# A hybrid decoder layer: convolution taps, rotary adds, state arithmetic and roots of the mixing phase on other engines

## The chip, the cores and the metric

The kernel runs on one core of one Trainium2 chip. A core has TensorE (PE in the profile, with its weight loads as PEld), VectorE (DVE), ScalarE (ACT), GpSimd (POOL) and SyncE (SP); in this kernel nearly all transfers are issued from SP's queue. The metric is device time of one execution in microseconds: the median of several runs.

## The reference

One layer of a decoder with two kinds of heads side by side, on 2048 tokens of width 1024, in fp32. Cut to what matters here:

```
mod = silu(c) @ w_ada + b_ada                     # six rows of 1024: shift, scale, gate, twice
h = modulate(rmsnorm(x, norm1_w), shift1, scale1)
q, k, v, z, xbc, dt_raw = split(h @ w_in)         # one projection, cut into column groups
q, k = rope(q), rope(k)                           # t1*cos - t2*sin, t2*cos + t1*sin
attn = sliding_window_attention(q, k, v, sinks)   # window 128
xbc = silu(causal_depthwise_conv(xbc))            # four taps along the tokens, plus a bias
dt = softplus(dt_raw + dt_bias); a = dt * A
# the state recurrence (SSD), by chunks of 128 tokens:
xdt = xs * dt
y = (C.B * decay) @ xdt + C @ state * exp(a_cs)   # within the chunk, and from the state before
state = state * exp(a_total) + B @ (xdt * exp(a_cs_end - a_cs))
y = (y + xs * d_skip) * silu(z)
y = y * rsqrt(mean(y*y over groups of 256) + eps) * ssm_norm_w
x = x + gate1 * (concat(attn, y) @ w_out)
x = x + gate2 * swiglu(modulate(rmsnorm(x, norm2_w), shift2, scale2))
out = rmsnorm(x, final_norm_w)
```

## The kernel before

**Tiles and precision.** The tokens are worked in four blocks of 512 (b = 0 to 3), each of four tiles of 128 (token 0 to token 3 of a block, below, are such tiles). Every fp32 product is made of three fp32r products (`mm3`, L270 to L272: high by high, high by low, low by high), so each operand is split in two. A weight comes raw from DRAM through SP, ACT rounds it to its high half (L262), GpSimd or VectorE subtracts (L263), and the split pair is stored for the later blocks (L266) which load it whole (L258). A normalized token operand is made by L319 (VectorE), L321 (ACT) and L322 (VectorE) into tiles named `hl`.

**Stages.** After an opening come, block by block, the projections: queries (rotary embedding, L372 to L375), keys and values, convolution (L474 to L485) and gate (L491, L492), each written out to DRAM. Beside the projections of block b+1 run the mixing generators of block b: `attentions` (per tile: transposes, scores, softmax, values) and `ssds` (per tile: the state recurrence). A function `tick` takes 1.1 steps of these side generators per step of the main ones. So block 0 is mixed while block 1 is projected, and block 1 while block 2 is. The output projection and the feed-forward layer (L951 to L953, L1090) follow.

**A convolution chunk** (8 per block, 128 channels by 512 tokens) takes its product from a bank `d` of PSUM. GpSimd copies the three columns of the halo in and out (L474, L476), ACT copies the product (L475) and makes two taps into two tiles `s` (L478 with the bias, L479), VectorE adds a tap to each (L480 from PSUM, L481 from SBUF), GpSimd adds the two (L482), ACT takes tanh (L483), VectorE makes the product (L484).

**A tile of the state recurrence.** `factors` makes the decay's two operands of 128x512 from a triangle and the steps, the high one on VectorE (L690), the low one on GpSimd (L692). The four token transposes land in PSUM bank `st`; VectorE reads it twice (L724 with the step, L725 with the skip weight); GpSimd makes the decayed tokens from the first of these (L726). L755 (VectorE) scales the old state's output, L756 (GpSimd) adds the skip; L766 (GpSimd) decays the state, L767 (VectorE) adds to it. L776 and L777 finish the tile, L781 (ACT) sums squares, and the root over groups of 256 is taken by `rsqrt` (tile `rs`, scratch `rss`): L237 and L238 on VectorE make a first guess by integer arithmetic, and three Newton rounds, with L240 to L245, follow on GpSimd in thirteen operations (on VectorE the same function takes nine, L248 to L250). L788 (ACT) scales the tile, and four PE transposes (L709) turn it. Bank `st` is one buffer, and PE's next use of it is L736.

**The adaLN rows.** Of the 48 columns of `mod`, 32 are made while the blocks run: a column is two halves of 256 KB, each loaded by L189 into one of two buffers `aw` and reduced by one VectorE operation (L195, with a small read of its accumulator).

**What sets the order.** PE's order is the order of the program (a manual schedule). The order of VectorE, ACT, GpSimd and SP is set by a scheduler that simulates the program with its own durations when the kernel is built; so a change of one operation's engine can move others in these queues. Each engine runs its queue in order, and a queue's head that waits holds what is behind it, on SP the loads too.

Of the kernel before, what the change touches and what calls it, by code (L numbers as in the profile page):

```python
# [11 lines left out]
F32 = mybir.dt.float32  # L12
# [5 lines left out]
P = 128  # L18
# [3 lines left out]
T = 512  # L22
# [21 lines left out]
def hymba_layer(ctx, tc, xT, crow, pos, wada, wadk, vecs, rows, wq, wkv, wz, wx, wo, wgu, wd, outT):  # L44
# [318 lines left out]

    def rope(dst, src, heads, gt, eng=nc.gpsimd):
        s4 = src.rearrange("p (h two j) -> p h two j", two=2, j=HALF)
        d4 = dst.rearrange("p (h two j) -> p h two j", two=2, j=HALF)
        tm = big("s", 3, pool=fw)[:, :heads * 64]
        t4 = tm.rearrange("p (h two j) -> p h two j", two=2, j=HALF)
        c = cos[:, gt, :].unsqueeze(1).broadcast_to([P, heads, HALF])
        s = sin[:, gt, :].unsqueeze(1).broadcast_to([P, heads, HALF])  # L370
        for i in range(2):
            nc.vector.tensor_tensor(d4[:, :, i, :], s4[:, :, i, :], c, ALU.mult)  # L372
            nc.vector.tensor_tensor(t4[:, :, i, :], s4[:, :, 1 - i, :], s, ALU.mult)
        for i, op in ((0, ALU.subtract), (1, ALU.add)):
            eng.tensor_tensor(d4[:, :, i, :], d4[:, :, i, :], t4[:, :, i, :], op)  # L375

# [47 lines left out]
    def first_columns(h):  # L424
# [15 lines left out]
        for t, ps in enumerate(kb):  # L440
            key_value(0, t, ps, nc.vector)
        for t, ps in enumerate(qb):
            q = extra.m2()
            rope(q, ps, 8, t, nc.vector)
            nc.sync.dma_start(q_d[t], q)

    def key_value(b, t, ps, eng=nc.gpsimd):
        kv = staged()
        rope(kv[:, 0:P], ps[:, 0:P], 2, b * NT + t, eng)
        nc.scalar.copy(kv[:, P:2 * P], ps[:, P:2 * P])  # L450
        nc.vector.tensor_tensor(dt_of[b][:, t, :], ps[:, 2 * P:2 * P + 8], dt_bias, ALU.add)
        nc.sync.dma_start(kv_d[b * NT + t], kv)
# [9 lines left out]
    def convolved(b, h):  # L462
        for c in range(8):
# [9 lines left out]
            cin = small([P, T + 3], "cin", 2, pool=ip)  # L473
            nc.gpsimd.tensor_copy(cin[:, 0:3], halo[:, c, :])  # L474
            nc.scalar.copy(cin[:, 3:T + 3], ps)  # L475
            nc.gpsimd.tensor_copy(halo[:, c, :], cin[:, T:T + 3])  # L476
            cv, th, o = big("s", 3, pool=fw), big("s", 3, pool=fw), big("sx", 2, pool=ip)
            nc.scalar.activation(cv, cin[:, 0:T], AF.Identity, scale=conv_w[:, c, 0:1], bias=conv_b[:, c:c + 1])  # L478
            nc.scalar.activation(th, cin[:, 1:1 + T], AF.Copy, scale=conv_w[:, c, 1:2])  # L479
            nc.vector.scalar_tensor_tensor(cv, ps, conv_w[:, c, 3:4], cv, ALU.mult, ALU.add)  # L480
            nc.vector.scalar_tensor_tensor(th, cin[:, 2:2 + T], conv_w[:, c, 2:3], th, ALU.mult, ALU.add)  # L481
            nc.gpsimd.tensor_tensor(cv, cv, th, ALU.add)  # L482
            nc.scalar.activation(th, cv, AF.Tanh)  # L483
# [21 lines left out]
    def steps(b):  # L505
# [27 lines left out]
        ex = small([P, 3, NT, 8], "ex", 1)  # L533
        nc.scalar.activation(ex.rearrange("p k t h -> p (k t h)"), ps[:, 0:96], AF.Exp)
        return dt, ahi, alo, ex

# [68 lines left out]
    def load_values(kv, slot):  # L605
        v = kv[:, P:2 * P].rearrange("p (r d) -> p r d", d=64)
        vhi, vlo = (v_ring[:, at:at + 256].rearrange("p (r d) -> p r d", d=P)[:, :, 0:64]
                    for at in (slot * 192, (2 + slot) * 192))
        nc.scalar.copy(vhi, v)
        nc.gpsimd.tensor_tensor(vlo, v, vhi.bitcast(F32), ALU.subtract)  # L610

# [61 lines left out]
    def ssds(b, stepping, m):  # L673
# [10 lines left out]
        ub = upper.unsqueeze(1).broadcast_to([P, 4, P])  # L684
        dst, out = spill[b], None

        def factors(t, g):
            hs, u = slice(4 * g, 4 * g + 4), m.m4()
            uhi, ulo = u[:, 0, :], u[:, 1, :]
            nc.vector.tensor_tensor(uhi.rearrange("p (h l) -> p h l", h=4), ub,  # L690
                                    ahi[:, t, hs].bitcast(F32).unsqueeze(2).broadcast_to([P, 4, P]), ALU.mult)
            nc.gpsimd.tensor_tensor(ulo.rearrange("p (h l) -> p h l", h=4), ub,  # L692
                                    alo[:, t, hs].unsqueeze(2).broadcast_to([P, 4, P]), ALU.mult)
            return uhi, ulo
# [20 lines left out]
        for t in range(NT):  # L715
# [9 lines left out]
            nc.vector.tensor_tensor(by_head(xsd), by_head(ps), bc64(d_skip), ALU.mult)  # L725
            nc.gpsimd.tensor_tensor(by_head(xdte), by_head(xdt), bc64(edte), ALU.mult)  # L726
            ps = bank("sm", 1)
# [21 lines left out]
            if old is not None:  # L749
# [5 lines left out]
                nc.vector.tensor_tensor(by_head(y), by_head(yo), bc64(ecs), ALU.mult)  # L755
                nc.gpsimd.tensor_tensor(y, y, xsd, ALU.add)  # L756
            else:
# [7 lines left out]
            if old is not None:  # L765
                nc.gpsimd.tensor_tensor(by_head(new), by_head(old), bc64(etot), ALU.mult)  # L766
                nc.vector.tensor_tensor(new, new, st, ALU.add)  # L767
# [16 lines left out]
            rs = small([P, 2], "rs", 2)  # L784
            rsqrt(rs, ss, 2, nc.gpsimd, "rss", sb)
            for g in range(2):
# [878 lines left out]
```

## Time and profile before

| | |
|---|---|
| median of 3 runs | 2269.98 us (2266.66 to 2273.71) |
| the profiled execution | 2267.25 us, span 2265.4 us |
| mean granted clock of TensorE | 0.986 |
| moved by DMA | 470.45 MB, 208 GB/s over the span |

In the profile's groups stand a line of the program, the engine, the operation, output<-input and shapes, the count, then busy us and mean ns of one, then the idle time of the engine just ahead of these instructions and what ended it. In the list of waits the columns are the waiting engine and line, the engine and line waited for, us in total, number of waits and the longest. In the timeline they are start, duration, engine and line, with the idle time before in brackets. Of the page, the engines' busy share in 40 slices of 56.6 us, in tenths, and the granted clock, show that the whole first third is uneven:

```profile
PE   6888988999999999999999999998999999999998
DVE  8987976774549887788787768987777775776565
POOL 2655533545123311144342222222333331110021
PEclk9988999999999999999999999999999999999998
```

The slices 2 to 13, from about 57 to 740 us, are the blocks' projections with the mixing beside them; what follows is the feed-forward layer.

### The profile page before, as it was taken

The numbers are of one execution on the slowest core, as the hardware profiler recorded it, in microseconds if no ns is written. First come the engines' busy times: TensorE is split into PE (matmuls) and PEld (weight loads), VectorE is DVE, ScalarE is ACT, GpSimd is POOL, SyncE is SP. The second block draws the span as 40 slices with busy tenths as digits, with TensorE's granted clock in tenths as the row PEclk, the third lists the DMA queues.
The fourth block names the chain that finished last, engine by engine and source line by source line (L and its number), as shares of the span: only waits on it lengthen the run. The fifth ranks groups of instructions, "written<-read, shape, count | busy, mean of one in ns | idle before, by whom it ended". The sixth has DMA issues, their size and how long they took to land. (4 is left out here: it accounts for less than half of the span.)

```text
span 2265.4 us, 33515 instructions
## 1 busy us (share of the span) xinstructions
PE 2166.4 (96%) x11072; PEld 1801.9 (80%) x11072; DVE 1681.7 (74%) x3147; ACT 1008.4 (45%) x2113; POOL 700.2 (31%) x806
## 2 busy tenths in 40 slices
PE   6888988999999999999999999998999999999998
PEld 5778788888978888888888877777888888788887
DVE  8987976774549887788787768987777775776565
ACT  4564543665345655433344444532333333554342
POOL 2655533545123311144342222222333331110021
PEclk9988999999999999999999999999999999999998
DMA  8898988788879523234335579977333335777553
GB/s 296 293 318 298 319 259 258 252 265 271 291 244 339 198 91 110 94 117 126 94 103 182 190 259 310 328 225 227 125 98 105 98 91 197 270 261 268 171 168 100
DMA packets 289325, 470.45 MB, mean 208 GB/s; under 512 B 27392, under 2 KB 97024, under 8 KB 289152
## 3 DMA queue, kind: packets, MB, share of 16 engines
q1 hardware_dynamic: 288576, 467.80, 62.4%
q8 instruction: 87, 1.43, 0.3%
q14 instruction: 86, 0.70, 0.1%
q10 hardware_dynamic: 576, 0.52, 0.1%
HBM read 335.50 MB, written 132.71 MB: 207 GB/s over the span
## 5 line engine op out<-in xcount | busy, mean ns | idle before, releaser
L1090 PE MATMUL d<-a,w 128*128 128x512 f32 x1716 | 405.6, 396 | 7.0 <-DVE a L1062 3.9
L1090 PEld LDWEIGHTS d<-a,w 128*128 128x128 f32 x1716 | 321.6, 188 | 87.8 <-DVE a L1062 5.7
L951 PE MATMUL d<-b,w 128*128 128x512 f32 x924 | 366.0, 400 | 4.4 <-ACT t L975 4.4
L953 PE MATMUL d<-b,w 128*128 128x512 f32 x924 | 366.8, 398 | 1.9 <-DVE w L843 1.9
L952 PE MATMUL d<-b,w 128*128 128x512 f32 x924 | 367.5, 398 | 0.0
L280 POOL TENSOR_TENSOR acc<-acc,t 128x512 f32<-128x512 f32 x70 | 106.2, 1518 | 404.4 <-ACT t L279 389.8
L951 PEld LDWEIGHTS d<-b,w 128*128 128x128 f32 x924 | 174.5, 189 | 44.6 <-ACT t L975 5.5
L842 ACT ACTIVATE w<-s 128x512 fp32r<-128x512 f32 x176 | 110.8, 632 | 221.5 <-PE d L953 174.3
L953 PEld LDWEIGHTS d<-b,w 128*128 128x128 f32 x924 | 174.5, 189 | 42.5 <-DVE w L843 2.6
L952 PEld LDWEIGHTS d<-b,w 128*128 128x128 f32 x924 | 174.9, 189 | 38.6
L270 PE MATMUL d<-w,hl 128*128 128x256 f32 (+1 forms) x592 | 175.8, 297 | 6.9 <-ACT hl L321 4.5
L272 PE MATMUL d<-w,hl 128*128 128x256 f32 (+1 forms) x592 | 171.4, 289 | 1.8 <-DVE hl L322 1.8
L271 PE MATMUL d<-w,hl 128*128 128x256 f32 (+1 forms) x592 | 171.1, 289 | 0.0
L270 PE MATMUL d<-hl,w 128*128 128x512 f32 x352 | 146.3, 416 | 4.3 <-ACT w L262 2.2
L843 DVE TENSOR_TENSOR w<-s,w 128x512 fp32r<-128x512 f32 x176 | 143.2, 815 | 8.6 <-ACT w L842 7.3
L1086 DVE TENSOR_TENSOR w<-raw,w 128x512 fp32r<-128x512 f32 x156 | 107.2, 696 | 53.6 <-ACT w L1085 53.4
L272 PE MATMUL d<-hl,w 128*128 128x512 f32 x352 | 140.5, 399 | 1.4 <-DVE w L263 0.7
L842 ACT ACTIVATE w<-raw 128x512 fp32r<-128x512 f32 x132 | 82.9, 630 | 130.4 <-PE d L953 59.1
L271 PE MATMUL d<-hl,w 128*128 128x512 f32 x352 | 139.6, 397 | 0.0
L1085 ACT ACTIVATE w<-raw 128x512 fp32r<-128x512 f32 x156 | 90.7, 588 | 102.7 <-PE d L1090 67.5
L1062 DVE TENSOR_TENSOR a<-a 128x512 fp32r<-128x512 f32 x154 | 107.5, 720 | 37.3 <-ACT a L1061 37.0
L1005 POOL TENSOR_TENSOR t<-t 128x512 f32<-128x512 f32 x44 | 75.3, 1712 | 180.5 <-DVE t L1004 124.1
(414 smaller groups left out, 5017.7 us busy)
## 6 DMA issues: line engine op xcount, KB each, us to landing
raw<-in_wgu_dram SPq DMA_DIRECT2D x176, 256.0 KB, 2.9
w<-w_x SPq DMA_DIRECT2D x48, 512.0 KB, 5.1
act_t<-t SPq DMA_DIRECT2D x88, 256.0 KB, 3.3
a<-act_t SPq DMA_DIRECT2D x88, 256.0 KB, 4.8
t<-in_xT_dram SPq DMA_DIRECT2D x80, 256.0 KB, 4.2
act_b<-t SPq DMA_DIRECT2D x66, 256.0 KB, 2.2
a<-act_b SPq DMA_DIRECT2D x66, 256.0 KB, 5.0
aw<-in_wada_dram SPq DMA_DIRECT2D x64, 256.0 KB, 4.5
```

The costliest lines, as they stand in the source:

```text
L270: nc.tensor.matmul(out, ahi, bhi, start=first, stop=False)
L271: nc.tensor.matmul(out, ahi, blo, start=False, stop=False)
L272: mm3.last = nc.tensor.matmul(out, alo, bhi, start=False, stop=last)
L280: eng.tensor_tensor(acc, acc, sq, ALU.add)
L842: nc.scalar.activation(hi, x, AF.Copy)
L843: eng.tensor_tensor(lo, x, hi.bitcast(F32), ALU.subtract)
L951: nc.tensor.matmul(out, ahi, bhi, start=first and k == 0, stop=False, skip_group_check=True)
L952: nc.tensor.matmul(out, ahi, blo, start=False, stop=False, skip_group_check=True)
L953: mm3.last = nc.tensor.matmul(out, alo, bhi, start=False, stop=k == 3, skip_group_check=True)
L1062: nc.vector.tensor_tensor(lo, raw, hi.bitcast(F32), ALU.subtract)
L1086: nc.vector.tensor_tensor(w[1], raw, w[0].bitcast(F32), ALU.subtract)
L1090: mm3.last = nc.tensor.matmul(ps, w[x][:, ws], act[k][y][:, ts], start=new and k == 0 and x + y == 0, stop=k == KP - 1 and x == 1, skip_gr ...
```

## The change

Work of the mixing phase moves from GpSimd to VectorE or ACT.

- Rotary adds (L375): all on VectorE; before, those of block 0's first columns only.
- Convolution: the halo copies move to ACT. ACT's second tap and GpSimd's add go; VectorE adds the two middle taps one after the other to the tile that holds the first and last. Only one `s` tile takes sums now, the other holds tanh.
- The value's low half (L610): VectorE.
- Decayed tokens: VectorE makes them from the transposes in PSUM instead of GpSimd from `xdt`; the decay factor is multiplied by the step beforehand, once per block (one small VectorE product).
- For blocks 0 and 1 only: the low factor is four ACT activations of 128x128 instead of a GpSimd product of 128x512; the skip add, the state's decay and the root are VectorE's.

```diff
-            eng.tensor_tensor(d4[:, :, i, :], d4[:, :, i, :], t4[:, :, i, :], op)
+            nc.vector.tensor_tensor(d4[:, :, i, :], d4[:, :, i, :], t4[:, :, i, :], op)
...
-            nc.gpsimd.tensor_copy(cin[:, 0:3], halo[:, c, :])
+            nc.scalar.copy(cin[:, 0:3], halo[:, c, :])
             nc.scalar.copy(cin[:, 3:T + 3], ps)
-            nc.gpsimd.tensor_copy(halo[:, c, :], cin[:, T:T + 3])
             cv, th, o = big("s", 3, pool=fw), big("s", 3, pool=fw), big("sx", 2, pool=ip)
             nc.scalar.activation(cv, cin[:, 0:T], AF.Identity, scale=conv_w[:, c, 0:1], bias=conv_b[:, c:c + 1])
-            nc.scalar.activation(th, cin[:, 1:1 + T], AF.Copy, scale=conv_w[:, c, 1:2])
+            nc.scalar.copy(halo[:, c, :], cin[:, T:T + 3])
             nc.vector.scalar_tensor_tensor(cv, ps, conv_w[:, c, 3:4], cv, ALU.mult, ALU.add)
-            nc.vector.scalar_tensor_tensor(th, cin[:, 2:2 + T], conv_w[:, c, 2:3], th, ALU.mult, ALU.add)
-            nc.gpsimd.tensor_tensor(cv, cv, th, ALU.add)
+            for i in (1, 2):
+                nc.vector.scalar_tensor_tensor(cv, cin[:, i:i + T], conv_w[:, c, i:i + 1], cv, ALU.mult, ALU.add)
             nc.scalar.activation(th, cv, AF.Tanh)
...
+        nc.vector.tensor_tensor(ex[:, 1], ex[:, 1], dt, ALU.mult)
...
-        nc.gpsimd.tensor_tensor(vlo, v, vhi.bitcast(F32), ALU.subtract)
+        nc.vector.tensor_tensor(vlo, v, vhi.bitcast(F32), ALU.subtract)
...
+        eng = nc.vector if b < 2 else nc.gpsimd
...
-            nc.gpsimd.tensor_tensor(ulo.rearrange("p (h l) -> p h l", h=4), ub,
-                                    alo[:, t, hs].unsqueeze(2).broadcast_to([P, 4, P]), ALU.mult)
+            if b < 2:
+                for i in range(4):
+                    nc.scalar.activation(ulo[:, i * P:(i + 1) * P], upper, AF.Copy,
+                                         scale=alo[:, t, 4 * g + i:4 * g + i + 1])
+            else:
+                nc.gpsimd.tensor_tensor(ulo.rearrange("p (h l) -> p h l", h=4), ub,
+                                        alo[:, t, hs].unsqueeze(2).broadcast_to([P, 4, P]), ALU.mult)
...
-            nc.gpsimd.tensor_tensor(by_head(xdte), by_head(xdt), bc64(edte), ALU.mult)
+            nc.vector.tensor_tensor(by_head(xdte), by_head(ps), bc64(edte), ALU.mult)
...
-                nc.gpsimd.tensor_tensor(y, y, xsd, ALU.add)
+                eng.tensor_tensor(y, y, xsd, ALU.add)
...
-                nc.gpsimd.tensor_tensor(by_head(new), by_head(old), bc64(etot), ALU.mult)
+                eng.tensor_tensor(by_head(new), by_head(old), bc64(etot), ALU.mult)
...
-            rsqrt(rs, ss, 2, nc.gpsimd, "rss", sb)
+            rsqrt(rs, ss, 2, eng, "rss", sb)
```

The changed kernel's line numbers differ by a few from L372 on: its taps from SBUF are L481, its tap from PSUM L479, its product after tanh L483, its decayed tokens L732, its turning transpose L715.

The scheduler orders the queues anew. Three places follow.

First, VectorE in the stretch where token 1 of block 0 takes its root while block 1 is projected; `rs` and `rss` are the root's tiles, `aw` an adaLN half, `t` and `hl` block 2's normalized operands. Before, after L238 the root is off VectorE:

```order
L661 TENSOR_TENSOR m_3455<-at,m_3454 128x4x128
L195 ISA aw,mod<-aw,csil,part 128x512
L195 ISA mod 128x1
L319 SCALAR_TENSOR_TENSOR t<-t,scl_147,bc 128x512
L238 TENSOR_SCALAR rs<-rss 128x2
L690 TENSOR_TENSOR m_3909<-upper,ahi 128x512
L195 ISA aw,part<-aw,csil,vec 128x512
L195 ISA part 128x1
```

Now:

```order
L238 TENSOR_SCALAR rs<-rss 128x2
L691 TENSOR_TENSOR m_3900<-upper,ahi 128x512
L481 SCALAR_TENSOR_TENSOR s<-cin,vec,s 128x512
L709 TENSOR_TENSOR m_3500<-m_3500,m_3431 128x512
L195 ISA aw,mod<-aw,csil,part 128x512
L195 ISA mod 128x1
L195 ISA aw,part<-aw,csil,vec 128x512
L195 ISA part 128x1
L248 TENSOR_TENSOR rss<-rs 128x2
L647 TENSOR_TENSOR ast<-ast 128x4
L481 SCALAR_TENSOR_TENSOR s<-cin,vec,s 128x512
L610 TENSOR_TENSOR v_ring<-m_2665,v_ring 128x2x64
```

The root's nine operations stand among others: up to the last of them (an L250) VectorE has six adaLN halves, four taps from SBUF (L481), four other wide operations and three small ones. From the L661 that began at 270.8 us in the profile to the first L661 of the second next pair, at 312.7 us, VectorE's order had 12 adaLN halves and has 19 now; up to that last L661, 51 of the 64 halves stood before, and 60 or 61 do now.

Second, SP's queue at the same place; w_z are the gate weights of block 1 in their split form, xs the convolution's results. Before:

```order
L566 DMA m_5081<-kv_190 128x256
L258 DMA w<-w_z_3_1853 128x2x512
L485 DMA xs_201<-sx 128x512
L189 DMA aw<-in_wada_dram 128x512 x2
L258 DMA w<-w_z_2_1941 128x2x512
L189 DMA aw<-in_wada_dram 128x512
L713 DMA mix_204<-m_3320 128x4x128
```

Now:

```order
L258 DMA w<-w_z_3_1845 128x2x512
L566 DMA m_5077<-kv_190 128x256
L189 DMA aw<-in_wada_dram 128x512
L484 DMA xs_201<-sx 128x512
L189 DMA aw<-in_wada_dram 128x512 x3
L484 DMA xs_201<-sx 128x512
L189 DMA aw<-in_wada_dram 128x512 x2
L719 DMA mix_204<-m_3316 128x4x128
L189 DMA aw<-in_wada_dram 128x512 x2
L258 DMA w<-w_z_2_1933 128x2x512
```

Between these two gate loads stood two adaLN half loads; now there are eight.

Third, VectorE at the root of token 3 of block 0, ahead of the rotary embedding of block 2 (L372, L373). Before:

```order
L777 SCALAR_TENSOR_TENSOR m_4062<-m_4062,m_3661 128x512
L783 TENSOR_SCALAR ss<-ss 128x2
L237 TENSOR_SCALAR rss<-ss 128x2
L238 TENSOR_SCALAR rs<-rss 128x2
L372 TENSOR_TENSOR so<-d,cos 128x4x32
```

Now:

```order
L789 TENSOR_SCALAR ss<-ss 128x2
L237 TENSOR_SCALAR rss<-ss 128x2
L238 TENSOR_SCALAR rs<-rss 128x2
L248 TENSOR_TENSOR rss<-rs 128x2
L249 SCALAR_TENSOR_TENSOR rss<-rss,ss 128x2
L250 SCALAR_TENSOR_TENSOR rs<-rss,rs 128x2
L248 TENSOR_TENSOR rss<-rs 128x2
```

The nine operations follow one another directly here, and the rotary products come after them.

More of the change, by code (lines that the diff above doesn't have):

```diff
@@ L362, in staged, with rope @@
         return small([P, 256], "so", 6, pool=ip)
-    def rope(dst, src, heads, gt, eng=nc.gpsimd):
+    def rope(dst, src, heads, gt):
         s4 = src.rearrange("p (h two j) -> p h two j", two=2, j=HALF)
@@ L440, in first_columns, with key_value @@
         for t, ps in enumerate(kb):
-            key_value(0, t, ps, nc.vector)
+            key_value(0, t, ps)
         for t, ps in enumerate(qb):
             q = extra.m2()
-            rope(q, ps, 8, t, nc.vector)
+            rope(q, ps, 8, t)
             nc.sync.dma_start(q_d[t], q)
-    def key_value(b, t, ps, eng=nc.gpsimd):
+    def key_value(b, t, ps):
         kv = staged()
-        rope(kv[:, 0:P], ps[:, 0:P], 2, b * NT + t, eng)
+        rope(kv[:, 0:P], ps[:, 0:P], 2, b * NT + t)
         nc.scalar.copy(kv[:, P:2 * P], ps[:, P:2 * P])
```

## The prediction

> **What bounds the kernel now.** I read the page's busy shares first, then the busy times by stage, then what TensorE waited for.
>
> ```profile
> span 2265.4 us, 33515 instructions
> PE 2166.4 (96%) x11072; PEld 1801.9 (80%) x11072; DVE 1681.7 (74%) x3147; ACT 1008.4 (45%) x2113; POOL 700.2 (31%) x806
> ```
>
> TensorE is busy for 96% of the span, so 2265.4 - 2166.4 = 99 us is all that any rearrangement of the other engines can win, apart from throttled clock. The stages tell where those lie (columns after the window: its length, busy us and count of PE, PEld, DVE, ACT, POOL, then granted clock, DMA share, GB/s):
>
> ```profile
> 100.00:150.00 50.00, 38.51 (x211) 31.71 (x210) 46.50 (x112) 37.95 (x86) 26.62 (x28) 0.90 0.92 321
> 150.00:214.00 64.00, 57.27 (x410) 54.72 (x409) 45.96 (x109) 30.06 (x72) 29.81 (x25) 0.87 0.90 301
> 237.00:270.50 33.50, 29.59 (x152) 23.39 (x150) 32.88 (x85) 20.62 (x48) 18.27 (x32) 1.00 1.00 336
> 270.50:296.10 25.60, 24.36 (x128) 20.30 (x129) 22.18 (x47) 13.81 (x30) 7.08 (x8) 0.93 0.78 252
> 296.10:312.40 16.30, 11.80 (x66) 10.02 (x66) 12.19 (x28) 7.43 (x19) 9.52 (x20) 0.90 0.66 211
> 414.00:492.00 78.00, 75.81 (x483) 65.74 (x483) 57.44 (x122) 51.02 (x126) 39.52 (x65) 1.00 0.69 228
> 492.00:765.00 273.00, 264.80 (x1610) 228.15 (x1609) 174.68 (x422) 136.21 (x332) 90.23 (x119) 0.99 0.83 281
> ```
>
> Before 312 us TensorE idles 11.5, 6.7, 3.9, 1.2 and 4.5 us in the five stages shown; from 492 to 765 us only 8.2 of 273. In the first three rows the DMA engines are 0.90 to 1.00 busy; from 237 to 270.5 VectorE is full too, 32.88 of 33.50 us. So in the stretch that the change touches, TensorE waits behind VectorE's queue or behind transfers. Its largest waits from 100 to 600 us:
>
> ```profile
> PE st L709 <- ACT m L788: 8.4, 2, 4.3
> PE at L584 <- DVE rsq L249: 3.9, 1, 3.9
> PE am L623 <- ACT m L587: 2.7, 1, 2.7
> PE at L623 <- DVE m L588: 2.2, 1, 2.2
> PE st L736 <- DVE m L725: 2.9, 2, 1.7
> ```
>
> L709 is the transpose of a finished token tile, behind the scaling by the root (L788): two stalls, for tokens 1 and 3 of block 0. Both follow a root that GpSimd works out.
>
> **The change part by part.** What leaves GpSimd, and what VectorE gets, per instruction:
>
> ```profile
> L482 POOL TENSOR_TENSOR s<-s 128x512 f32<-128x512 f32 x30 | 42.4, 1415 | 69.1 <-DVE s L481 52.3 <-DVE ast L641 10.5 <-DVE rstd L250 6.2
> L480 DVE SCALAR_TENSOR_TENSOR s<-d,vec,s 128x512 f32<-128x512 f32 x29 | 21.5, 742 | 4.3 <-ACT s L478 4.3
> L481 DVE SCALAR_TENSOR_TENSOR s<-cin,vec,s 128x512 f32<-128x512 f32 x30 | 24.3, 810 | 4.1 <-ACT s L479 4.1
> L372 DVE TENSOR_TENSOR so<-d,cos 128x128 f32<-128x128 f32 x48 | 13.3, 278 | 11.2 <-PE d L272 11.2
> L724 DVE TENSOR_TENSOR m<-st,dtv 128x512 f32<-128x512 f32 x10 | 6.8, 681 | 0.1
> L651 ACT ACTIVATE m<-m,ast 128x128 f32<-128x128 f32 x8 | 2.6, 390 | 0.7 <-DVE ast L648 0.7
> ```
>
> A convolution chunk loses its 1.42 us GpSimd add and its ACT tap and gets one more VectorE tap of 0.74; 32 chunks are 24 us more for VectorE. The 76 rope adds of the later blocks cost at most 0.28 each, 21 us. The decayed tokens (16), and for two blocks the skip add (7) and state decay (7), cost 0.68 each, 20 us. The value residual (16 by 0.28), the product of decay and step (4 small ones) and eight roots of nine small operations (0.17 each, below) are some 17 us. Together about 82 us move to an engine that is full from 237 to 270.5 us but has 20.6 us free from 414 to 492 and 98 from 492 to 765. So the price is where VectorE is already behind. ACT gives up 32 taps and takes the low factors of two blocks, 16 products of 128x512, as 64 activations of L651's shape, 0.39 each or 25 us, and 64 copies of three columns; at 37.95 busy of 50 us and 20.62 of 33.50 it can hold them, and four in a row keep a waiting normalized operand (hl) at most 1.6 us. I take 0, with 2 above.
>
> *237 to 312 us.* The rows that bear it, of VectorE from 270.5 to 312.4 us, and of the ring of adaLN halves (two buffers of 256 KB, L189 loads, L195 reduces) from 237 to 352 us:
>
> ```profile
> L195 DVE CUSTOM_DVE_ANT_0 aw<-aw,csil,vec 128x512 f32<-128x512 f32 x6 | 4.4, 742 | 0.5 <-DMA aw<-in_wada_dram 0.5
> L481 DVE SCALAR_TENSOR_TENSOR s<-cin,vec,s 128x512 f32<-128x512 f32 x3 | 2.2, 744 | 2.6 <-ACT s L479 2.6
> L777 DVE SCALAR_TENSOR_TENSOR m<-m,m 128x512 f32<-128x512 f32 x1 | 1.8, 1762 | 0.0
> L642 DVE TENSOR_TENSOR ast<-row,ast 128x4 f32<-128x4 f32 x1 | 1.3, 1272 | 0.0
> L189 SPq DMA_DIRECT2D aw<-in_wada_dram x31: 327/333/612, 237.8 to 345.3; - x31
> DMA to landing us min/median/max: 2.6/4.2/6.3
> DVE aw L195 <- DMA aw<-in_wada_dram: 9.7, 7, 3.3
> ```
>
> Between the residuals of the transposed probabilities (L661) that start at 270.8 and 312.7 us, the new VectorE order holds 19 halves instead of 12, seven more taps, one more gated product of the convolution of 0.68, one decayed-token product, one state decay, the value residual and a root's nine operations: 7 x 0.74 + 7 x 0.74 + 3 x 0.68 + 0.28 + 9 x 0.17 = 14.2 us. VectorE was busy 22.18 + 12.19 = 34.4 of 41.9 us there. What comes back is the stretch of operations that ran beside GpSimd: L777 at 1.76 where the others of its size take 0.74, and L642 at 1.27 for four numbers where the small operations below take 0.15, together 2.1. That makes 46.5 us of work for 41.9, 4.6 over. The ring gives a second count: a buffer is refilled in 4.2 us and reduced in 0.74, so with two a half comes every 2.47 us, and 19 take 47.0 us, 5.1 over. A third is the root of token 1:
>
> ```profile
> 298.92 0.15 DVE L238 TENSOR_SCALAR rs<-rss 128x2 int32<-128x2 int32 x1
> 305.64 0.20 POOL L245 TENSOR_TENSOR rs<-rss,rs 128x2 f32<-128x2 f32 x1
> 306.44 0.87 PE L709 MATMUL st<-ident,m 128*128 128x128 f32 x4 [4.35 <-ACT m L788]
> ```
>
> On GpSimd it took 305.84 - 299.07 = 6.8 us after L238. In the new VectorE order there stand, between L238 and the root's last operation, six halves, four taps, four other wide operations and three small ones beside the nine: 7.4 + 2.8 + 0.7 + 1.5 = 12.4 us, 5.6 more, and TensorE stands at L709 for it. A half that has not landed holds the root behind it, and with it the value residual, the taps and the next L661, for whose results TensorE waits next. The three counts are one delay seen three times; I take +5.2. Bounds: 0, if halves land in 2.6 us (19 x 1.67 = 32 us) and the gaps hold the rest; +15, if landing lies halfway from median to maximum (5.25; 19 x 3.0 = 57 us). The stretch from 237 to 270.5, with DMA at 1.00, I leave at 0.
>
> *After 312 us* the halves pulled forward are missing where they stood before: VectorE's 9.7 us of waits for them shrink, since the new order has 61 of 64 halves done at the later of those two L661, the old one 51. TensorE's waits from 312 to 352 us were these:
>
> ```profile
> PE st L762 <- DVE m L755: 1.4, 1, 1.4
> PE sm L698 <- DVE m L731: 1.3, 1, 1.3
> PE st L736 <- DVE m L725: 1.2, 1, 1.2
> ```
>
> I take all 3.9 as won (bounds 0 and 3.9).
>
> *Token 3's root* stands compact in both orders:
>
> ```profile
> 364.80 0.17 DVE L237 TENSOR_SCALAR rss<-ss 128x2 int32<-128x2 int32 x1
> 365.00 0.17 DVE L238 TENSOR_SCALAR rs<-rss 128x2 int32<-128x2 int32 x1
> 368.29 0.19 POOL L245 TENSOR_TENSOR rs<-rss,rs 128x2 f32<-128x2 f32 x1
> 368.51 0.91 ACT L788 ACTIVATE m<-m,rs 128x256 f32<-128x256 f32 x2 [3.95 <-POOL rs L245]
> 369.00:372.00 3.00, 2.92 (x14) 2.82 (x15) 0.00 (x0) 1.56 (x6) 0.00 (x0) 0.51 0.00 0
> 177.00:180.00 3.00, 2.67 (x12) 2.47 (x13) 0.75 (x1) 0.00 (x0) 0.00 (x0) 0.57 1.04 366
> 177.04 0.39 PE L270 MATMUL d<-w,hl 128*128 128x256 f32 x1 [2.44 <-ACT hl L321]
> ```
>
> From L238's end the GpSimd steps took 368.48 - 365.17 = 3.3 us; nine VectorE steps at 0.20 (from L237 to L238) take 1.8: 1.5 less. The stall of 4.1 us also halved the clock for the 3 us after it (0.51), 1.5 us of work. Whether a stall of 2.6 us still does is told by 177.04: a wait of 2.44 was followed by a clock of 0.57. So I keep that loss and take -1.5 (bounds -1.5 and -3.0). The Trainium skill ("TensorE: Matmul & The Clock Gate", Part 1) gives an idle window of about 3.4 us ahead of the drop; by it the clock would hold and the term be -3.0, but the row at 177 us differs, and the measurement decides.
>
> *Decayed tokens.* L726 read SBUF; its successor is the third reader of bank st, so the bank's next use, L736, gets it 0.6 us later. It was late twice (2.9 us): +1.2, with 0 below and, if all eight tiles of two blocks were, 5 above.
>
> *100 to 237 us.* The convolution's GpSimd link is gone and L481 loses 0.07 us of stretch, but VectorE is 46.50 of 50 busy to 150 us, the DMA engines 0.92: -2 (bounds 0 and -4). *After 370 us*: some 30 us of added work (16 taps, 48 rope adds, the residuals) against the 20.6 and 98 free; if that cover failed, the rope adds alone would show up to 0.28 x 48 = 13 us. I take 0, with 3 either way.
>
> Sum: -2 + 5.2 - 3.9 - 1.5 + 1.2 + 0 = **-1.0 us**. The profiled execution took 2267.25, 2.7 under the median of 2269.98; the shift goes on the median: **2269.0 us**.
>
> **The rivals.** *Faster: the link and the stretch were the path.* For it speaks that VectorE idled 2.6 us for ACT's tap L479, which is gone, and that a four-number operation took 1.27 us. Ring 0, TensorE's idle 5.7 us from 270.5 to 312.4 down by 4; half of the 8.8 us of waits at L584 and L623 gone; the 3.9 won; token 3 at -3.0: -4 - 4.4 - 3.9 - 3.0 + 1.2 = -14.1, **2256**. Against it: the added work is larger than the stretch in the one stage where both can be counted. The Trainium skill ("SBUF — State Buffer", "SBUF: two separate sides") has VectorE operations with two SBUF inputs and GpSimd ones exclude each other for a whole instruction. The trace agrees in kind (L481 810 ns beside 742 for the PSUM reader L480), and by it alone this rival would be the forecast.
>
> *Slower: the adaLN halves pulled ahead block VectorE.* If a half comes every 3.0 us, the ring costs +15, and half of the later waits stay: 15 - 2 - 2 - 1.5 + 1.2 = +10.7, **2281**. It decides from about 2.8 us per half on (19 x 2.8 - 41.9 - 4.3 = 7.0). For it: landing took up to 6.3 us, and SP's new order has eight half loads between two gate reloads; against it, the DMA share is only 0.66 to 0.78 there.
>
> *The change does nothing to TensorE*, since GpSimd's work was hidden and its waits only change their names: **2270**.
>
> **How the numbers follow.** What differs by less than 0.3%, 6.8 us, cannot be told from no change here. Near zero 0.38 (0.28 within the bound, 0.07 faster, 0.03 slower); the faster rival 0.31 (0.29 beyond it); the slower 0.23 (0.21 beyond); nothing 0.08 (all within). So faster 0.36, same 0.40, slower 0.24. The likeliest case's own range is 2260 to 2277; the whole, with a tenth left out on each side, 2253 to 2283.
>
> **What would show it.** Right: TensorE's wait at the turning transpose (L709 before) near 10 us for token 1 and near 2.6 for token 3; VectorE above 95% busy, or waiting for halves, from 296 to 316 us; few waits from 330 to 352. The L661 of 312.7 us would start 3 to 6 us later, and the lag be gone by 375. The faster rival: the waits at L584 and L623 halved, that L661 not later. The slower: halves more than 2.8 us apart. Wrong altogether: a change of more than 3 us after 400.

## The result

The changed kernel is slower: median 2294.19 us (2289.48 to 2297.68), beside 2269.72 us for the kernel before, a ratio of 1.0105 with a 95% interval of 1.0081 to 1.0130. The forecast was 2269.0, no change, with an upper bound of 2283.

The head of the profile after, its first two lines:

```profile
span 2293.6 us, 33441 instructions
PE 2177.2 (95%) x11072; PEld 1813.7 (79%) x11072; DVE 1723.8 (75%) x3377; ACT 1013.9 (44%) x2209; POOL 517.3 (23%) x468
```

GpSimd lost 183 us of work (700.2 to 517.3). VectorE gained 42 us, though 82 were counted for what moved to it. Part of the difference is that operations that stayed got shorter, by some 23 us in sum, with less of GpSimd beside them (the convolution's gated product, 822 ns before, takes 716); the rest is mostly that neighbours overlap in the profile, which a sum of durations counts twice. TensorE did the same 11072 matmuls in 2177.2 us instead of 2166.4, and idled 116.4 us instead of 99.0. So of the 28.2 us between the two profiled executions (24.5 between the medians), 17.4 are longer waits and 10.8 longer matmuls, which go with the lower clock (a mean of 0.976 instead of 0.986).

Where this happened is told by windows cut at the same matmuls (the first count in each row). Before, at edges chosen in its time:

```profile
187.00:237.00 50.00, 45.81 (x327) 42.22 (x326) 43.56 (x126) 23.92 (x61) 36.71 (x43) 0.93 0.86 292
237.00:296.00 59.00, 53.85 (x280) 43.59 (x279) 54.96 (x131) 34.43 (x78) 25.25 (x39) 0.97 0.90 299
296.00:312.40 16.40, 11.90 (x67) 10.12 (x66) 12.29 (x28) 7.43 (x19) 9.62 (x20) 0.90 0.66 211
312.40:351.00 38.60, 34.67 (x280) 33.66 (x280) 29.46 (x62) 13.60 (x33) 12.63 (x21) 1.00 0.90 285
351.00:589.00 238.00, 230.41 (x1524) 205.57 (x1523) 147.44 (x372) 120.86 (x308) 110.92 (x179) 0.99 0.79 259
680.00:773.00 93.00, 88.95 (x548) 76.80 (x547) 81.29 (x156) 59.21 (x133) 33.72 (x34) 0.98 0.87 299
```

After, the same stretches of work:

```profile
186.20:247.50 61.30, 50.04 (x328) 46.62 (x327) 54.30 (x167) 26.73 (x71) 21.01 (x15) 0.81 0.75 249
247.50:299.40 51.90, 51.41 (x279) 42.42 (x278) 49.85 (x138) 31.58 (x85) 0.00 (x0) 1.00 0.94 322
299.40:322.40 23.00, 12.60 (x66) 10.90 (x65) 18.98 (x54) 10.95 (x32) 0.00 (x0) 0.78 0.78 245
322.40:357.30 34.90, 34.32 (x280) 33.58 (x279) 22.52 (x59) 12.76 (x33) 0.00 (x0) 1.00 0.75 243
357.30:602.30 245.00, 234.55 (x1525) 209.02 (x1524) 168.91 (x477) 127.18 (x351) 40.22 (x30) 0.98 0.77 253
695.00:798.60 103.60, 93.34 (x548) 80.38 (x547) 89.84 (x168) 56.29 (x138) 18.78 (x14) 0.93 0.77 265
```

In order, the stretches are +11.3, -7.1, +6.6, -3.7, +7.0 and +10.6 us; the rest of the program adds 3.5. That rest hides two large parts: the lag behind the kernel before falls from 25.6 us at 773 us to 22.3 at 1300, and grows by 7 again by 1600. The change has no operation there: the mixing of the last blocks runs on to about 1240 us, and the last moved operation is a decayed-tokens product (L732) at 1224 us. Before and after:

```profile
1300.00:1600.00 300.00, 287.08 (x1217) 228.49 (x1215) 241.87 (x384) 120.60 (x212) 79.08 (x46) 0.99 0.80 264
```

```profile
1322.30:1629.30 307.00, 288.10 (x1216) 228.03 (x1215) 246.44 (x389) 121.41 (x212) 81.69 (x46) 0.99 0.79 259
```

Where TensorE lost 11.3 us, VectorE had 10.7 us more to do; where it won 7.1, VectorE had 5.1 less. Of TensorE's largest waits from 60 to 900 us after the change, the second and third had been 1.5 us and nothing:

```profile
PE st L715 <- ACT m L794: 11.5, 2, 9.0
PE d L270 <- DVE s L373: 8.7, 3, 6.2
PE d L270 <- DVE s L479: 6.2, 1, 6.2
PE am L623 <- ACT m L587: 5.7, 1, 5.7
```

L715 and L794 are the old L709 and L788. L373 and L479 (L480 before) are the last VectorE readers of a bank `d` of PSUM that the next product needs.

The wait of 9.0 us is token 1's root, in the timeline of VectorE and TensorE:

```profile
302.23 0.17 DVE L238 TENSOR_SCALAR rs<-rss 128x2 int32<-128x2 int32 x1
307.67 0.75 DVE L195 CUSTOM_DVE_ANT_0 aw<-aw,csil,part 128x512 f32<-128x512 f32 x1 [0.80 <-DMA aw<-in_wada_dram]
312.28 0.75 DVE L195 CUSTOM_DVE_ANT_0 aw<-aw,csil,part 128x512 f32<-128x512 f32 x1 [0.91 <-DMA aw<-in_wada_dram]
314.36 0.16 DVE L250 SCALAR_TENSOR_TENSOR rs<-rss,rs 128x2 f32<-128x2 f32 x1
315.62 1.11 PE L715 MATMUL st<-ident,m 128*128 128x128 f32 x4 [9.05 <-ACT m L794]
```

From L238's end to the root's end are 12.1 us, in which VectorE stood still twice for a half that had not landed. The wait at 222 us shows something else; VectorE, then GpSimd, then TensorE with its clock:

```profile
210.93 1.37 DVE L375 TENSOR_TENSOR so<-so,s 128x128 f32<-128x128 f32 x1
212.22 1.28 DVE L647 TENSOR_TENSOR ast<-ast 128x4 f32<-128x4 f32 x1
215.21 1.38 DVE L375 TENSOR_TENSOR so<-so,s 128x128 f32<-128x128 f32 x1
216.51 1.81 DVE L691 TENSOR_TENSOR m<-upper,ahi 128x512 fp32r<-128x512 f32 x1
218.25 1.35 DVE L375 TENSOR_TENSOR so<-so,s 128x128 f32<-128x128 f32 x1
219.51 1.81 DVE L195 CUSTOM_DVE_ANT_0 aw<-aw,csil,part 128x512 f32<-128x512 f32 x1
221.93 0.28 DVE L373 TENSOR_TENSOR s<-d,sin 128x128 f32<-128x128 f32 x1
210.45 1.69 POOL L280 TENSOR_TENSOR acc<-acc,t 128x512 f32<-128x512 f32 x1 [1.35 <-ACT t L279]
212.10 1.38 POOL L263 TENSOR_TENSOR w<-raw,w 128x528 fp32r<-128x528 f32 x1
214.60 1.84 POOL L280 TENSOR_TENSOR acc<-acc,t 128x512 f32<-128x512 f32 x1 [1.12 <-ACT t L279]
216.40 1.37 POOL L263 TENSOR_TENSOR w<-raw,w 128x528 fp32r<-128x528 f32 x1
222.35 0.56 PE L270 MATMUL d<-w,hl 128*128 128x264 f32 x1 [6.18 <-DVE s L373]
222.00:225.00 3.00, 2.65 (x12) 2.68 (x13) 3.00 (x12) 3.00 (x8) 1.16 (x1) 0.50 0.66 185
```

A rotary add of 0.28 us takes 1.35 to 1.38 where it starts beside one of GpSimd's sums of squares (L280): the adds at 210.93 and 215.21 us end 0.16 and 0.15 us after the L280 that ran beside them. Beside the weight splits (L263), a VectorE operation on four numbers (L647) takes 1.28. The multiply that frees the bank (L373) stands behind three such adds and three other stretched operations (L647, L691, L195). TensorE waits 6.18 us and then runs at half its clock (0.50). At 745 us it is a tap:

```profile
734.86 0.75 DVE L868 SCALAR_TENSOR_TENSOR t<-t,scl,sm 128x512 f32<-128x512 f32 x1 [1.98 <-DMA t<-mid]
744.32 0.75 DVE L479 SCALAR_TENSOR_TENSOR s<-d,vec,s 128x512 f32<-128x512 f32 x1
745.12 0.58 PE L270 MATMUL d<-w,hl 128*128 128x256 f32 x1 [6.22 <-DVE s L479]
```

L868 and its like prepare the feed-forward layer's operands; VectorE works without a gap from 734.86 to L479 and past it.

### The profile page after: what moved, and what is told of

It reads as the page before. It is cut to its first block, busy times and chain, and to the rows that moved or that the text cites. A ratio compares the mean times of both kernels' runs of the same rounds, so it can differ in the third digit from the quotient of the medians.

```text
span 2293.6 us, 33441 instructions
## 1 busy us (share of the span) xinstructions
PE 2177.2 (95%) x11072; PEld 1813.7 (79%) x11072; DVE 1723.8 (75%) x3377; ACT 1013.9 (44%) x2209; POOL 517.3 (23%) x468
## 5 line engine op out<-in xcount | busy, mean ns | idle before, releaser
L280 POOL TENSOR_TENSOR acc<-acc,t 128x512 f32<-128x512 f32 x70 | 106.8, 1525 | 653.3 <-ACT t L279 644.0
L270 PE MATMUL d<-w,hl 128*128 128x256 f32 (+1 forms) x592 | 181.7, 307 | 18.4 <-DVE s L373 7.6
L272 PE MATMUL d<-w,hl 128*128 128x256 f32 (+1 forms) x592 | 176.5, 298 | 4.6 <-DVE hl L322 4.6
L271 PE MATMUL d<-w,hl 128*128 128x256 f32 (+1 forms) x592 | 176.3, 298 | 0.0
L270 PE MATMUL d<-hl,w 128*128 128x512 f32 x352 | 146.1, 415 | 3.6 <-ACT w L262 1.5
L272 PE MATMUL d<-hl,w 128*128 128x512 f32 x352 | 140.3, 399 | 0.8 <-POOL w L263 0.7
L270 PEld LDWEIGHTS d<-w,hl 128*128 128x128 f32 x592 | 121.8, 206 | 22.3 <-issue 9.3
```

The source lines that it names most:

```text
L270: nc.tensor.matmul(out, ahi, bhi, start=first, stop=False)
L271: nc.tensor.matmul(out, ahi, blo, start=False, stop=False)
L272: mm3.last = nc.tensor.matmul(out, alo, bhi, start=False, stop=last)
L280: eng.tensor_tensor(acc, acc, sq, ALU.add)
```

## The experiments

Eighteen kernels, each timed against the kernel before on one chip. Ratios are to that kernel, with 95% intervals; the changed kernel's is 1.0105 (1.0081 to 1.0130).

**1. The adaLN halves.** The first theory was that the halves pulled ahead hold up all else. The edit gives 36 of the 64 halves another place:

```diff
-        with tc.issue_after(last_fetched.ins):       # SP: the loads
+        with tc.issue_after((load_x.last if late else last_fetched).ins):
...
-        with tc.issue_after(first_done.ins):         # VectorE: the reduces
+        with tc.issue_after((modulated.last if late else first_done).ins):
```

`late` holds from the 15th column on; the two anchors are block 3's last operand load and its last L322.

> The changed kernel with 36 of the 64 adaLN halves queued behind block 3's normalized operands on VectorE and SP (28 stay early), so that none stands in VectorE's order from 215 to 500 us. The adaLN theory (halves hold up the root and the bank releases): token 1's wait of 9.05 us falls to 4 or less, the wait of 6.2 us at 222 us mostly goes, 10 to 16 us come back, 2278 to 2284. The bank theory (added VectorE work itself stands ahead of the operations that free banks of PSUM): only token 1's excess of 5 to 6 us comes back, 2287 to 2290, and the waits of 6.2 us at 222 and 745 us stay.

> The kernel before with the same 36 adaLN halves moved behind block 3's operands. The adaLN theory: VectorE's 9.7 us of waits for halves from 237 to 352 us go and with them 4 us of TensorE's waits there, 2262 to 2266. The bank theory: nothing that can be told, 2266 to 2273, since TensorE's two waits for roots on GpSimd stay at 4 us each.

Measured: the changed kernel so 2291.91 us, 1.0105 (1.0085 to 1.0126); the kernel before so 2266.87, 0.9998 (0.9985 to 1.0011). The end does not move, but the way there does. The kernel before from 187 to 351 us, the same work with the halves gone, then the stretch of block 3, before and with the halves in it:

```profile
187.00:351.00 164.00, 146.23 (x948) 129.59 (x947) 140.26 (x344) 79.38 (x189) 84.21 (x121) 0.96 0.87 285
```

```profile
187.70:331.90 144.20, 139.00 (x947) 125.51 (x947) 113.78 (x270) 78.31 (x187) 77.73 (x121) 0.99 0.77 258
```

With 26.5 us less on VectorE, TensorE does the same 947 matmuls in 19.8 us less. It loses most of it between 540.6 and 768.3 us, where the halves stand now: 227.7 us for what took 213.1. In the changed kernel the lead over its former self is 11 us at 351 us, as the adaLN theory says, and then goes in the same way. To find a cheaper place, the anchors were set to block 2's last step addition (L451), in both kernels:

> The kernel before with 36 adaLN halves queued behind block 2's last step addition (398 us before), so that they run from about 400 to 520 us, where VectorE had a quarter of its time free. With the halves behind block 3's operands, TensorE ran 19 us ahead of the kernel before at 350 us and lost that from 570 to 770 us, where the halves stood instead. If the place of the halves is what costs, most of these 19 us stay: 2250 to 2256. If the 570 to 770 us stretch loses time for another reason (a lead runs into a transfer or a load that does not come earlier), nothing stays: 2264 to 2270.

> The changed kernel with the same 36 halves from about 400 to 520 us. If the halves' place and the change's added VectorE work cost separately, this is 11 to 15 us under the changed kernel and 20 to 30 above the kernel before in the same order of halves: 2276 to 2282. If the change costs only because it pulls the halves ahead, it meets that kernel: 2250 to 2260.

Measured: 2267.28, 0.9998 (0.9988 to 1.0008), and 2299.15, 1.0140 (1.0125 to 1.0155). Both expectations of a gain missed; the second kernel is some 8 us slower than the changed one. The stretch in which the halves then stand, before and with them:

```profile
351.00:492.00 141.00, 134.72 (x912) 120.52 (x911) 94.93 (x254) 75.02 (x198) 66.36 (x115) 0.99 0.75 245
```

```profile
334.40:491.00 156.60, 141.82 (x914) 125.47 (x913) 125.33 (x317) 75.91 (x197) 71.84 (x115) 0.95 0.84 276
```

VectorE was busy for two thirds of this stretch, and with 30 us more on it TensorE took 15.6 longer. Spreading the halves does not help either (each column queued behind the newest result of the projections, from about 500 to 780 us):

> The kernel before with 36 adaLN halves queued one column at a time behind results of the projections, so that they are spread from about 500 to 780 us. Packed behind block 3's operands they cost 13 us from 570 to 770 us after 19 had been won; packed behind block 2's step addition they cost 13 from 410 to 480. If packing is what costs, half of the 19 us stays: 2255 to 2262. If each half costs TensorE about 0.5 us wherever VectorE is busy beside it, nothing stays: 2264 to 2270.

Measured: 2267.83, 0.9996 (0.9980 to 1.0012); the lead of 19 us is gone by 700 us. Last, the 36 halves on other engines:

```diff
+            nc.gpsimd.tensor_tensor(w, w, csil[:, hs], ALU.mult)
+            nc.scalar.activation(w, w, AF.Copy, scale=0.5, accum_out=sums_of[:, j:j + 1])
```

> The kernel before with 36 adaLN halves multiplied on GpSimd and summed by ACT, 27 us less on VectorE in the stretch before 350 us. If VectorE's queue is what TensorE waits for there, 5 to 15 us faster, 2252 to 2262. If the exclusion between VectorE and GpSimd gives it back (each product of 1.3 us on GpSimd holds up VectorE's operations on SBUF), no change or slower, 2265 to 2275.

Measured: 2270.00, 1.0002 (0.9991 to 1.0013). A product takes GpSimd 1405 ns (31 of them in that stretch), and the lead at 351 us is 4.5 us instead of 19, lost by 370. This is the second reading of that expectation: over the same 947 matmuls VectorE is busy for 133.4 us instead of 140.3, only 6.8 less, since the operations that stayed on it got longer (the gated product 1044 ns instead of 815).

So the adaLN theory falls as an account of the end. What the stretches show instead is a price: a us more or less of VectorE's busy time went with 0.75 us of TensorE's time (19.8 for 26.5), 0.58 (14.6 for 25.3, where the halves stood from 540.6 us on), 0.52 (15.6 for 30.4) and 0.66 (4.5 for 6.8), also where VectorE has a third of its time free. In the first three the loads of the halves moved along with the reduces, so the price is of both; only in the last did the loads stay.

**2. One part alone.** Each kernel is the one before with a part of the change's diff and nothing else.

> The kernel before with the rotary adds of all blocks on VectorE and nothing else. The bank theory (adds stand in VectorE's queue ahead of the multiplications that free a bank): TensorE waits again for L373 near 222 us, 4 to 10 us slower, 2272 to 2278. If it takes several parts together to fill VectorE, it is within 3 us of before: 2265 to 2270.

> The kernel before with the convolution's taps and halo copies as changed and nothing else. The bank theory: the tap from PSUM (L479 here) stands behind the two new taps of the chunk before, TensorE waits for it near 745 us, 4 to 9 us slower, 2271 to 2277. If it takes several parts together: 2265 to 2270. If GpSimd's link in the convolution was the path: 2255 to 2263.

> The kernel before with only the part for blocks 0 and 1: low factors on ACT, skip add, state decay and root on VectorE. With rope alone at +5 us and the convolution alone at about +1, the change's 24 us leave some 18. If the parts add up, this part has most of it: 2278 to 2286, with token 1's wait at the turning transpose near 9 us. If it is their sum on VectorE's queue that costs (each alone finds room), it is within 5 us of before: 2265 to 2273, and token 3's wait near 2.5 us.

> The kernel before with only the roots of blocks 0 and 1 on VectorE. The root theory (nine operations of a dependent chain stand among others in VectorE's queue): token 1's wait is 7 us or more, token 3's near 2.5 us, 2270 to 2275. If the root is held only where the other parts have filled VectorE, token 1's wait is 5 us or less and the time 2264 to 2269.

> The kernel before with only the value residual and the decayed tokens on VectorE. If the third reader of bank st costs what the prediction said, TensorE's waits at the bank's next use (L736 before) grow from 2.9 to 4 or 5 us, 2268 to 2271. If the parts add up and the two blocks' part is cheap, this one is dear: 2275 or more.

> The kernel before with the convolution as changed and, for blocks 0 and 1, the low factors on ACT and the skip add and state decay on VectorE; rotary adds, value residual, decayed tokens and roots stay on GpSimd. The parts that cost nothing singly: if they are free together, 2265 to 2270; if relieving GpSimd pays once the dear parts are left out, 2255 to 2264; if it is the sum of work on VectorE (24 of 38 us of it before 350) that costs, 2273 to 2280.

| part alone | median us | ratio |
|---|---|---|
| rotary adds | 2273.49 | 1.0025 (1.0011 to 1.0039) |
| convolution | 2268.98 | 0.9998 (0.9989 to 1.0007) |
| blocks 0 and 1 (factors, skip, state, root) | 2267.78 | 0.9999 (0.9986 to 1.0012) |
| root of blocks 0 and 1 | 2275.14 | 1.0032 (1.0022 to 1.0043) |
| value residual and decayed tokens | 2277.12 | 1.0040 (1.0025 to 1.0055) |
| convolution, and blocks 0 and 1 without the root | 2272.36 | 1.0017 (1.0007 to 1.0027) |

The rotary adds bring the wait for L373 at 222 us by themselves (7.0 us), and the time is 6 us longer, as the bank theory expected. The convolution brings the wait for L479 (4.4 us) and at 770 us lies 9 us behind; but it gets 3 us back by 1300 us and 3 more by 1600, so the forecast of 4 to 9 us missed. The root is the sharpest case. Alone it makes token 1's wait 10.0 us, together with the other parts for two blocks 3.9, from 295 to 330 us:

```profile
PE st L710 <- ACT m L789: 10.0, 1, 10.0
```

```profile
PE st L715 <- ACT m L794: 3.9, 1, 3.9
```

In the first, VectorE's order scatters the nine operations (12.4 us from L238's end to the last); in the second, seven of them stand together and it takes 8.1. The expectation that a part which holds the root costs at least what the root does was wrong: where the scheduler puts the nine decides. The last row, the convolution with most of the blocks' part, both free alone, costs 4 us (2 to 6), between what its readings expected.

**3. One part undone.** The changed kernel with a part put back.

> The changed kernel with the rotary adds of the later blocks back on GpSimd, all else as changed. The bank theory: the wait of 6.2 us for L373 at 222 us goes, and the half clock after it, 7 to 10 us come back, 2284 to 2287. The adaLN theory: the halves are pulled ahead as before, token 1's wait stays near 9 us, at most 3 us come back, 2291 to 2294.

> The changed kernel with the convolution as it was (halo copies and one add on GpSimd, two taps on ACT). The bank theory: the wait of 6.2 us for L479 at 745 us goes, with its half clock 9 us come back, and VectorE is 5 us freer from 270 to 312, so 9 to 14 in all, 2280 to 2285. The adaLN theory: the halves are still pulled ahead, 3 to 5 us, 2289 to 2291.

> The changed kernel with the roots of blocks 0 and 1 back on GpSimd, which has nothing else to do from 250 to 400 us. The root theory: token 1's wait falls from 9.05 to 3 to 5 us, token 3's returns from 2.5 to 4, so 3 to 7 us come back, 2287 to 2291. If token 1 is late because all of VectorE's queue is, its wait stays at 7 us or more and the time at 2292 to 2296.

> The changed kernel with the value residual and the decayed tokens back on GpSimd. If the 9 us that this part cost by itself are its own, they come back: 2283 to 2287. If they came from the order that the scheduler found with it (most of that lag arose after 1300 us, where the change has no operation), the result is elsewhere: within 3 us of the changed kernel, 2291 to 2297.

> The changed kernel with both the rotary adds of the later blocks and the roots of blocks 0 and 1 back on GpSimd. Singly they gave back some 8 and 12 us. If they are two separate losses, together 20: 2270 to 2277. If either alone already takes VectorE's queue off the path, together no more than 13: 2280 to 2284.

| put back | median us | ratio | us below the changed kernel, by the ratios |
|---|---|---|---|
| rotary adds | 2284.19 | 1.0074 (1.0047 to 1.0101) | 7 |
| convolution | 2289.17 | 1.0090 (1.0067 to 1.0114) | 3 |
| root | 2282.57 | 1.0057 (1.0039 to 1.0076) | 11 |
| value residual and decayed tokens | 2281.30 | 1.0050 (1.0033 to 1.0066) | 12 |
| rotary adds and root | 2280.30 | 1.0046 (1.0030 to 1.0063) | 13 |

These runs were on several chips, so the last column goes by the ratios; each of its figures is uncertain by 7 to 8 us. The intervals of the first two rows overlap the changed kernel's, so their gain is not clear of noise. The root and the value part gave back more than either of their readings expected.

With the rotary adds back, the wait for L373 is not among TensorE's from 187 to 330 us, but token 1's is 10.4. With the root back, token 1's is 2.8, and the wait for L373 is 7.3. Both back give 13 us where the two singly sum to 18, a difference within the noise; so whether the parts are separate losses cannot be told from the ends. Done alone, the parts sum to some 14 us of the 24: 6 for the rotary adds, 9 for the value part, and next to nothing for the other two (the root is in the third).

The stretches tell more than the ends. In the kernels that leave the halves in place, the time for the same matmuls, less that of the kernel before (one profiled execution each), was:

| stretch, in the time of the kernel before | part | on VectorE, us | not moved, us |
|---|---|---|---|
| 187 to 237 us | rotary adds | +4.7 to +11.2 (6 kernels) | -0.9 to +5.4 (7) |
| 296 to 312 us | root | +3.0 to +7.8 (7) | -2.3 to -1.0 (6) |
| 680 to 773 us | convolution | +7.4 to +10.7 (8) | -2.0 to +2.2 (5) |
| 1300 to 1600 us | value residual, decayed tokens | +7.1 to +11.4 (7) | -3.1 to +0.2 (6) |

So in the last three stretches the loss comes and goes with one part, whatever else is changed. In the first, putting the rotary adds back takes the changed kernel's loss from 11.2 us (11.3 by the rounded edges above) to 5.4; the other half comes with other parts, of which the convolution, the blocks' part and the value part alone cost 3.5 to 5.3 us there.

**4. The named operation or the queue.** The rotary adds stay on VectorE, but behind the multiplications that free the banks:

```diff
+            with tc.issue_after(rope.last.ins):      # the last multiplication of the tiles
+                for i, op in ((0, ALU.subtract), (1, ALU.add)):
+                    nc.vector.tensor_tensor(d4[:, :, i, :], d4[:, :, i, :], t4[:, :, i, :], op)
```

> The changed kernel with the same rotary adds on VectorE, but queued behind the multiplications of all four tiles that free the two banks (for keys and values, of both tiles). The bank theory: the wait of 6.2 us for L373 at 222 us falls to 2 us or less and 3 to 8 us come back, 2286 to 2291. If the adds cost by their time beside GpSimd (1.37 us each there instead of 0.28) wherever they stand, at most 2 us come back, 2292 to 2295.

Measured: 2293.31, 1.0100 (1.0084 to 1.0117). The wait for L373 went, as meant, and TensorE's waits from 187 to 250 us begin with another:

```profile
PE am L270 <- DVE m L685: 8.8, 1, 8.8
```

L685 is here the residual of the transposed probabilities (L661). What had stood in front of the bank's readers stands in front of this now: four of the adds take 5.28 us, from 211.30 us on, beside GpSimd. So the bank theory falls too, and the second reading, that the adds cost their time beside GpSimd wherever they stand, fits (2292 to 2295). At 222 us VectorE's queue as a whole is late, and whichever of its results TensorE needs next shows the wait; moving the adds within the queue gives nothing back, while without them the stretch lost 5.4 us instead of 11.2.

**What stays open.** The value residual and decayed tokens cost 7 to 11 us between 1300 and 1600 us, where the change has no operation: with the part alone the lag behind the kernel before grows from 2.1 to 10.4 us there, and without it in the changed kernel it does not grow (16.3 to 15.1). How the part does it is not shown. TensorE's waits for the operand that L818 makes are 1.0 us in the kernel before, 3.6 in the changed kernel and none in the one with the part put back; the order of the feed-forward layer's operations differs there, and which pair of them does it was not tried. No kernel here beats the one before by more than its interval.

## Why the prediction was wrong

By its own steps:

- **"After 370 us ... I take 0"**, with 3 either way: this step failed, and by most. The lag grew from 8.4 us at 370 to 28.2 at the end. VectorE's free time was taken as cover for some 30 us of added work. It was free by the average, 147 of 238 us busy from 351 to 589, but it works off its queue in order, and TensorE waits for results inside that queue. The convolution's added tap (L481) delays the tap that frees a bank: 10.6 us from 680 to 773, of which 3.3 came back by 1300. Another 7 us came from 1300 to 1600 with the value residual and decayed tokens, by a cause that stays open. The prediction's own sign for "wrong altogether", more than 3 us after 400 us, came true: the lag was 9.1 there.
- **"100 to 237 us ... -2"** had the wrong sign: measured -0.8 to 187 us and +11.3 in the 50 us after it. The step named VectorE's 46.50 of 50 us and the DMA share of 0.92 as what bounds the stage, took a small gain from the convolution, and charged nothing for the rotary adds there. From 187 us on the DMA engines were 0.86 busy before and 0.75 after, and VectorE 43.56 of 50 us. VectorE had idled 18 us from 150 to 214 us, but mostly ahead of 187, which was no room for work that comes after. A rotary add was priced at 0.28 us from rows that read PSUM; most took that, but the three ahead of the bank's release, with two operands in SBUF beside GpSimd's sums of squares, took 1.37.
- **"237 to 312 us ... +5.2"**: the root's delay held by size, +6.6 in the stretch with token 1. The root took 12.1 us after L238 where 12.4 was counted, TensorE's wait was 9.05 where near 10 was forecast. The 7.1 us won just ahead of it were not foreseen, so the whole term came to about 0. There TensorE's wait of 3.5 us for a normalized operand (L270 behind L321, at 271.6 us before) is gone, and the DMA engines were 0.94 busy; that the lag of 10 us had let loads come ahead is likely, not shown.
- **"After 312 us ... all 3.9 as won"**: -3.7 to 351 us.
- **"Token 3's root ... -1.5"**: right for the wait (2.49 us instead of 4.1), and the clock as the row at 177 us had it. The lag still grew from 351 to 370 us, by 2.1, with a new wait of 2.12 us at 361 us, and was not gone by 375. After, VectorE, TensorE and the clock behind it:

```profile
375.23 0.17 DVE L238 TENSOR_SCALAR rs<-rss 128x2 int32<-128x2 int32 x1
377.00 0.16 DVE L250 SCALAR_TENSOR_TENSOR rs<-rss,rs 128x2 f32<-128x2 f32 x1
377.81 0.84 PE L715 MATMUL st<-ident,m 128*128 128x128 f32 x4 [2.49 <-ACT m L794]
378.00:381.00 3.00, 3.00 (x19) 2.80 (x19) 0.00 (x0) 1.30 (x5) 0.00 (x0) 0.69 0.11 38
```

A wait of 2.49 us is followed by a clock of 0.69. By the Trainium skill ("TensorE: Matmul & The Clock Gate", Part 1) an idle window of about 3.4 us goes ahead of the drop; this case has it after 2.44 and 2.49 us of waiting.

- **"Decayed tokens ... +1.2"**: the bank's next use waited 0.8 us in all instead of 2.9, so the third reader cost nothing there. The part, with the value residual, cost 9 us alone, nearly all of it after 1300 us.
- **The slower rival** had the sign, and with 2281 lay nearer, but not the cause: the halves were not what decided, as the first group of runs shows. Its price of 3.0 us per half did not occur (from 307.67 to 312.28 us two halves more began, 2.3 us each). **The faster rival** was right that the stretch of operations is large, some 23 us of VectorE's time, and wrong that its end frees the path. The Trainium skill ("SBUF — State Buffer", "SBUF: two separate sides") says that VectorE operations with two SBUF inputs and GpSimd ones that read SBUF shut each other out for a whole instruction. The rotary adds that ended just after GpSimd's L280 agree, and they speak against this change: an operation moved to VectorE meets what GpSimd kept.
- **The clock** was left out of every term but one. 10.8 of the 28.2 us are longer matmuls; the rows behind the waits of 6.18 and 2.49 us show clocks of 0.50 and 0.69.

## What to carry to other kernels

Free time on an in-order engine is not cover for more work on it when another engine waits for results inside its queue: here 30 us more on a VectorE two thirds busy went with 15.6 us more for TensorE. Read such an engine's room in the stretch after its last long wait, not in a stage's average, and price a moved operation by one with the same kind of operands beside the same neighbour. When moving an operation behind a named wait only brings up the next wait, the queue is late, and work has to leave it. And compare kernels stretch by stretch at the same matmuls: here that told which part cost where, when the ends could not.

## What the runs showed of the hardware that was not expected

A VectorE add of 128x128 with both operands in SBUF took 1.35 to 1.38 us when it began beside a GpSimd addition of 128x512 (1.69 and 1.84 us), about five times its 0.28, and ended 0.15 to 0.16 us after it. TensorE's granted clock fell to 0.50 to 0.69 in the 3 us after waits of 2.49, 6.18 and 9.05 us, and 10.8 of the 28 us between the two profiled executions were longer matmuls. In the kernel before, thirty-six reduces of 0.74 us could be put at four places and on two sets of engines without moving the end by 3 us, though 20 us came and went on the way.
